# A two-layer encoder trunk in float32 on one NeuronCore: end keys first in the linear attention, opening weight sums begun at the fetch, the last input pair in two parts, and weight pairs in groups of three, four and four

## The chip, the core and the metric

The kernel runs on one core of a Trainium2 chip. TensorE (PE) multiplies, VectorE (DVE), ScalarE (ACT) and GpSimd (POOL) do the element-wise work, SyncE (SP) and POOL issue transfers. The metric is the device time of one execution in microseconds (us), all weights being read from HBM in that time.

## The reference

Two layers, each made of a feed-forward block, a mixer and a second feed-forward block, on 512 tokens plus 16 meta tokens (T = 528; the last feed-forward block has 512):

```python
for l in range(DEPTH):
    h = h + 0.5 * swiglu(rmsnorm(h, norm_gains[l, 0]), ffn_w_gate[l, 0], ffn_w_up[l, 0], ffn_w_down[l, 0])
    h = h + mixer(rmsnorm(h, norm_gains[l, 1]), w_in[l], ...)
    h = h + 0.5 * swiglu(rmsnorm(h, norm_gains[l, 2]), ffn_w_gate[l, 1], ffn_w_up[l, 1], ffn_w_down[l, 1])
return rmsnorm(h, final_norm)[:, N_META:]

def swiglu(x, w_gate, w_up, w_down):
    return (jax.nn.silu(x @ w_gate) * (x @ w_up)) @ w_down
```

The model width is 1024, the hidden width 2816. One half of the mixer is a gated linear attention (GLA) in two directions d, with 4 heads of 64 keys. It needs, for each direction, the running sum `bcum` of the log gates within a chunk, and from it three decayed copies of queries and keys:

```python
q_dec = qc * jnp.exp(bcum)
k_inv = kc * jnp.exp(-bcum)
k_end = kc * jnp.exp(btot - bcum)
kv_chunk = jnp.einsum('bhnjd,bhnjv->bhndv', k_end, vc)
```

`k_end` are the end keys of the title. The other half of the mixer is softmax attention, and both are merged by gates.

## The kernel before, in words

**Data.** `h` stays in SBUF, as 8 chunks of 128 features by 528 tokens. All weights are float32; each 128x1024 weight tile is split into a rounded part `whi` (ACT, L238) and a rest `wlo` (DVE, L239), and each product of a weight tile is three matmuls (hi by hi, hi by lo, lo by hi). A matmul of 264 tokens takes 0.122 us where PE doesn't wait.

**Feed-forward block.** The text calls the four blocks ffn(0,0), ffn(0,1), ffn(1,0), ffn(1,1) (layer, place in the layer); in names they read `_00_`, `_01_`, `_10_`, `_11_`. The 2816 hidden features are 11 "pairs" of 256. Gate and up projection of a pair are made by a Strassen-like scheme: the weights are cut in blocks 11, 12, 21, 22 and the inputs in two halves of the features and two of the tokens; seven products, named "1" to "7", of 24 matmuls each take the place of eight. Products 1, 2 and 4 use blocks 11, 12 and 22 as they are. The others use sums of blocks, made by transfers that add: s3 (for product 7) is the negative of block 11 (ACT, L189) plus block 21; s2 (product 6, the tile `w22`) is block 22 plus s3; s1 (product 5, the tile `w21`) is block 21 plus block 22; s4 (product 3) is the negative of block 12 plus s2. The adds are issued by POOL (L194), strictly one behind the other; an add that waits holds the queue behind it. Plain loads are issued by SP, in order as well. s1 and s2 have 2 buffers (`wsb`), s3 and s4 have 3 (`wsa`), raw weights 3, `whi` and `wlo` 4 each. Weights are split 4 tiles ahead of use (`make`) and loaded 6 ahead (`fetch`); the sums of a pair are ordered when its block 11 ("1") and 12 ("2") are split (`sums`, L196).

**Inputs of a block.** Each two chunks of the input form an input pair with 7 positions in `xc` (`Norm.pair`, L475), in the order of PLACE: products 1, 2, 5, 6, 7, 4, 3. Position 0 and 1 are plain halves, the others sums and differences made by DVE and split by ACT and DVE. The fourth pair (chunks 6, 7) is the last to come, since the previous phase makes the chunks of `h` in order (`add_to_h`, L529: two DVE operations, L527 and L536, or one, L532).

**Order of the products.** `ffn_steps` (L51) writes it by hand, by groups of pairs GROUPS. A block that isn't the first opens with products 1 and 2 of pair 0 together (step O, `two_products`, L566, with the last input pair left for the end), then products 1 and 2 of pair 1, then 6, 5, 7, 4, 3 of pair 0, and 6, 5 of pair 1 between. Behind each group come the down products of its hidden tiles (step D, L404), for 8 output chunks m; the last group's down products end the block, and after each the chunk m is added to `h` and handed to the next phase's norm. The row norm `rs` is got beside the opening and is needed first when hidden values are made. Which operation stands first on an engine is then decided by a scheduler that follows the program order and priorities.

**Linear attention.** `gla_pair` (L699) runs four times (2 layers, 2 pairs of heads), each for d = 0 and 1: a matmul z on PE (L721), Abs, Exp and Ln on ACT, the gate (DVE, L727), the running sum (DVE scan, L731), differences with the chunk's middle and end (L739 to L742), four exponentials on ACT, then three products on DVE and one on POOL: `qp` (L757), `kp` on POOL (L758), the end keys `ke` (L760), and the queries `qin` (L777). PE transposes `ke` (L764, L765); behind that DVE copies it (L767, L769). PE fills the time with the projections of the next tiles (L404), which stand between z and the transposes in its queue.

Of the kernel before, what the change touches and what calls it, by code (L numbers as in the profile page):

```python
# [17 lines left out]
P = 128  # L18
# [21 lines left out]
O_QB, O_KB, O_VB, O_GA, O_GB = 1568, 2080, 2208, 2336, 3360  # L40


GROUPS = (4, 4, 3)
HELD = 4
LATE = KC - 3
PLACE = {p: i for i, p in enumerate("1256743")}
# [112 lines left out]
class Weights:  # L159
# [32 lines left out]
    def add(self, t, src):  # L192

        self.nc.gpsimd.dma_start(t, src, accum_op=ALU.add)  # L194

    def sums(self, f, i, product, w):  # L196


        got = self.summed
        if product == "1":  # L200
            s3 = self.negative(f, i, "s3", w)
            self.add(s3, self.dram(f, i, "21"))
            s2 = self.block(f, i, "22", self.short, "wsb")
            self.add(s2, s3)
            got[f, i, "7"], got[f, i, "6"] = s3, s2
        else:
            s1 = self.block(f, i, "21", self.short, "wsb")
            self.add(s1, self.dram(f, i, "22"))
            s4 = self.negative(f, i, "s4", w)
            self.add(s4, got[f, i, "6"])  # L210
            got[f, i, "5"], got[f, i, "3"] = s1, s4
# [12 lines left out]

    def make(self, upto):
        nc = self.nc
        while self.made < min(upto, len(self.loads)):
            self.fetch(self.made + 1)
            s = self.made
            load = self.loads[s]  # L230
            w = self.raws.pop(s, None)
            if w is None:
                w = self.summed.pop(load)
            hi = self.hi_pool.tile([P, SLAB], F32R, tag="whi", name=f"whi{s}")
            lo = self.lo_pool.tile([P, SLAB], F32R, tag="wlo", name=f"wlo{s}")
            for a in np.split(np.arange(SLAB), 2 if s == 0 else 1):
                cs = slice(a[0], a[-1] + 1)
                nc.scalar.copy(hi[:, cs], w[:, cs])  # L238
                nc.vector.tensor_tensor(lo[:, cs], w[:, cs], hi[:, cs].bitcast(F32), ALU.subtract)  # L239
            self.got[s] = (hi, lo)  # L240
            self.got.pop(s - 12, None)
            self.made += 1
            if not isinstance(load, int) and load[2] in ("1", "2"):
                self.sums(*load, w)

    def use(self, j):
# [26 lines left out]
def build(tc, ctx, xt, wts, win, par, w2, const, umask, out):  # L273
# [7 lines left out]
        return ctx.enter_context(tc.tile_pool(name=name, bufs=bufs, space=space))  # L281

    one = pool("one", 1)
    slots = {n: pool("s_" + n, b) for n, b in dict(g=16, t=6, rs=2).items()}
# [68 lines left out]
    def v2(ap):  # L353
        return ap.rearrange("p (a b) -> p a b", a=2)
# [81 lines left out]
    class Norm:  # L436
# [38 lines left out]
        def pair(self, j):  # L475
# [15 lines left out]
            if not begun:  # L491
                parts(0, b11)
                parts(1, b21)
            S.activation(hi[:, 6], b22, AF.Copy, scale=-1.0)
            V.scalar_tensor_tensor(lo[:, 6], b22, -1.0, hi[:, 6].bitcast(F32), ALU.mult, ALU.subtract)
# [4 lines left out]
            V.tensor_tensor(t34[:, :w], b12, b22, ALU.subtract)  # L500
            V.tensor_tensor(t34[:, w:], b21, t12[:, w:], ALU.subtract)
            parts(slice(4, 6), v2(t34))

        def chunk(self, c):
# [12 lines left out]

# [22 lines left out]
    def ffn(l, f, norm, done, following):  # L540
# [25 lines left out]
        def two_products(p, names):  # L566
# [132 lines left out]
    def gla_pair(l, p, lr, w2t, sr, qa, ka, va, n_out):  # L699
# [17 lines left out]
        for d in range(2):  # L717
# [13 lines left out]
                V.tensor_tensor_scan(c[:, bs], ones.broadcast_to([P, n]), g[:, bs], 0.0, ALU.mult, ALU.add)  # L731
            mid = blk(c)[:, :, 63:64].broadcast_to([P, NB, P])
            tot = blk(c)[:, :, 127:128].broadcast_to([P, NB, P])
            mm_, mt_ = c[:, T - 1 : T].broadcast_to([P, META]), None
            src = c
            if d == 1:
                V.tensor_tensor(g, c, g, ALU.subtract)
                src = g
            V.tensor_tensor(blk(a), blk(src), mid, ALU.subtract)  # L739
            V.tensor_tensor(a[:, MB], src[:, MB], mm_, ALU.subtract)  # L740
            V.tensor_tensor(blk(ct_), blk(src), tot, ALU.subtract)
            V.tensor_copy(ct_[:, MB], a[:, MB])  # L742
            r16 = 1.0 / 16.0
            qp, kp = slot("p"), slot("p")
            if d == 0:
                S.activation(g, a, AF.Exp, scale=-r16)
                S.activation(a, a, AF.Exp, scale=r16)
                S.activation(c, c, AF.Exp, scale=r16)
                S.activation(ct_, ct_, AF.Exp, scale=-r16)
                ein, eq, ek, eend = c, a, g, ct_  # L750
            else:
                S.activation(c, a, AF.Exp, scale=-r16)
                S.activation(a, a, AF.Exp, scale=r16)
                S.activation(ct_, ct_, AF.Exp, scale=-r16)
                S.activation(g, g, AF.Exp, scale=r16)
                ein, eq, ek, eend = ct_, c, a, g
# [3 lines left out]
            V.tensor_tensor(ke, ka, eend, ALU.mult)  # L760

            tp = pair()
            for b, bs, _ in blocks:
                TE.transpose(tp[:, 0, bs], ke[:, bs], ident)  # L764
            TE.transpose(tp[:META, 1, :P], ke[:, MB], ident)  # L765
# [258 lines left out]
        norm.pools = open_pools("right", **{"x": dict(x=16), "xc": dict(xc=8)}[kind])  # L1024

    def block_pools():
        pools = open_pools("left", wsa=3, wsb=2)
        W.long, W.short = pools["wsa"], pools["wsb"]
        return pools

    def decay_weights(l):

        w, low = slot("t")[:, :512], slot("t")[:, :512]
        wt = one.tile([P, 512], F32R, tag="w2", name=nm("w2"))
        S.dma_start(w, w2[l])
        S.copy(wt, w)
        V.tensor_tensor(low, w, wt.bitcast(F32), ALU.subtract)
# [24 lines left out]
    def mixer(l, norm, done, following):  # L1062

        x, n_out = norm.x, T if l < DEPTH - 1 else SEQ
        pools = open_pools("left", e=8, i=5, p=7, q=6, k=5, lr=1)
# [210 lines left out]
```

## Time and profile before

| | us |
|---|---|
| median of three runs | 2263.21 |
| the three runs | 2260.45, 2263.21, 2268.38 |
| the profiled execution | 2263.49 |
| its span (first to last instruction) | 2261.6 |
| PE busy | 2204.5 (97%) |
| DVE busy | 1527.2 (68%) |
| ACT busy | 1218.3 (54%) |
| POOL busy | 164.7 (7%) |
| moved by transfers | 312.85 MB, 138 GB/s |

PE is busy nearly all the time, the other engines are not. The columns of the views are: start, duration, engine, line, operation, tiles; the bracket at the end of a row holds the idle time of that engine just before, and what ended it. The clock is shown as a share of full speed (1.00).

### The profile page before, as it was taken

The page shows a single profiled execution, that of the slowest core. Times are in us where ns is not written, and L with a number is a line of the kernel's source. Part 1 is how long each engine was busy: PE and PEld are TensorE (multiplying, and loading weights), DVE is VectorE, ACT ScalarE, POOL GpSimd, SP SyncE. Part 2 cuts the span into 40 slices and gives each one's busy share as a digit, 9 for nine tenths or more (in the row PEclk, how much of TensorE's full clock was granted, in tenths as well). Part 3 has the DMA queues.
Part 4 walks back from the last instruction along what each step waited for, and adds up shares of the span by engine and source line. Part 5 has one row for each costly group of instructions (what it writes and reads, how often), then busy time and mean ns, then how long its engine had stood idle before and what let it go on. Part 6 is the DMA issues. An engine that isn't in the chain of part 4 may idle for free. (4 is left out here: it accounts for less than half of the span.)

```text
span 2261.6 us, 39885 instructions
## 1 busy us (share of the span) xinstructions
PE 2204.5 (97%) x16538; PEld 2102.9 (93%) x16538; DVE 1527.2 (68%) x2397; ACT 1218.3 (54%) x1824; POOL 164.7 (7%) x184
## 2 busy tenths in 40 slices
PE   8999999999999999999979999999999999999998
PEld 8999999989999999999979999998888888989897
DVE  7657567577876666565676565575789767756565
ACT  8536355344784564453565363454557836636354
POOL 1011000000000010101011010100000000101010
PEclk9999999999999999999999999999999999999999
DMA  8778463211113485867658585732121135869661
GB/s 239 188 177 212 134 168 108 75 57 57 48 38 113 124 203 154 197 174 173 180 139 207 139 217 149 178 105 87 56 68 54 47 121 152 215 155 225 156 181 66
DMA packets 87542, 312.85 MB, mean 138 GB/s; under 512 B 9664, under 2 KB 11840, under 8 KB 87360
## 3 DMA queue, kind: packets, MB, share of 16 engines
q1 hardware_dynamic: 60816, 217.67, 28.6%
q0 software_dynamic: 24768, 90.19, 22.5%
q8 instruction: 130, 2.13, 0.4%
q10 hardware_dynamic: 1776, 2.43, 0.3%
q14 instruction: 52, 0.43, 0.1%
HBM read 263.07 MB, written 2.10 MB: 117 GB/s over the span
## 5 line engine op out<-in xcount | busy, mean ns | idle before, releaser
L597 PE MATMUL ss<-xc,whi 128*128 128x264 f32 (+1 forms) x4720 | 865.1, 285 | 16.9 <-ACT whi L238 9.5
L597 PEld LDWEIGHTS ss<-xc,whi 128*128 128x128 f32 x4720 | 734.7, 189 | 19.7 <-ACT whi L238 10.3
L597 PE MATMUL ss<-xc,wlo 128*128 128x264 f32 (+1 forms) x2360 | 671.4, 285 | 5.1 <-DVE wlo L239 5.1
L404 PE MATMUL ss<-g,whi 128*128 128x264 f32 (+1 forms) x2620 | 482.8, 300 | 0.0
L597 PEld LDWEIGHTS ss<-xc,wlo 128*128 128x128 f32 x2360 | 446.8, 189 | 6.4 <-DVE wlo L239 6.3
L404 PEld LDWEIGHTS ss<-g,whi 128*128 128x128 f32 x2620 | 380.6, 188 | 15.7
L404 PE MATMUL mm<-x,whi 128*128 128x264 f32 (+1 forms) x1712 | 385.8, 315 | 0.0
L238 ACT CAST whi<-w 128x1024 fp32r<-128x1024 f32 (+1 forms) x220 | 230.0, 1046 | 266.2 <-PE ss L404 116.1
L239 DVE TENSOR_TENSOR wlo<-w,whi 128x1024 fp32r<-128x1024 f32 (+1 forms) x220 | 266.6, 1218 | 116.1 <-ACT whi L238 114.8
L238 ACT CAST whi<-raw 128x1024 fp32r<-128x1024 f32 x190 | 199.2, 1048 | 260.2 <-PE ss L597 89.8
L239 DVE TENSOR_TENSOR wlo<-raw,whi 128x1024 fp32r<-128x1024 f32 x190 | 232.1, 1222 | 105.8 <-ACT whi L238 104.8
L404 PE MATMUL ss<-g,wlo 128*128 128x264 f32 (+1 forms) x1310 | 302.2, 300 | 0.0
L404 PEld LDWEIGHTS mm<-x,whi 128*128 128x128 f32 x1712 | 281.2, 190 | 15.3 <-DVE x L393 0.2
L404 PE MATMUL mm<-x,wlo 128*128 128x264 f32 (+1 forms) x856 | 265.2, 314 | 0.0
L404 PEld LDWEIGHTS ss<-g,wlo 128*128 128x128 f32 x1310 | 209.2, 188 | 8.3
L239 DVE TENSOR_TENSOR wlo<-s,whi 128x1024 fp32r<-128x1024 f32 x86 | 105.1, 1222 | 95.7 <-ACT whi L238 95.6
L238 ACT CAST whi<-s 128x1024 fp32r<-128x1024 f32 x86 | 90.3, 1050 | 146.9 <-PE ss L597 128.3
L404 PEld LDWEIGHTS mm<-x,wlo 128*128 128x128 f32 x856 | 161.2, 190 | 7.6
L527 DVE SCALAR_TENSOR_TENSOR t<-ss,rs 128x528 f32<-128x528 f32 (+1 forms) x93 | 64.6, 700 | 126.4 <-PE ss L404 126.3
L189 ACT ACTIVATE s<-w 128x1024 f32<-128x1024 f32 x86 | 91.2, 1060 | 81.7 <-DMA w<-win 46.5
L194 POOL DMA_DIRECT2D w<-win x43 | 37.8, 880 | 599.3 <-DVE wlo L239 222.3
L393 DVE TENSOR_TENSOR g<-c,g 128x528 fp32r<-128x528 f32 (+1 forms) x88 | 61.5, 699 | 22.6 <-ACT g L392 22.6
(280 smaller groups left out, 2829.6 us busy)
## 6 DMA issues: line engine op xcount, KB each, us to landing
w<-win SPq DMA_DIRECT2D x218, 512.0 KB, 4.7
raw<-wts SPq DMA_DIRECT2D x190, 512.0 KB, 3.3
w<-win POOLq DMA_DIRECT2D x43, 512.0 KB, 6.8
s<-win POOLq DMA_DIRECT2D x43, 512.0 KB, 6.7
w<-s POOLq DMA_DIRECT2D x43, 512.0 KB, 5.9
s<-w POOLq DMA_DIRECT2D x43, 512.0 KB, 7.0
h<-xt SPq DMA_DIRECT2D x3, 528.0 KB, 7.6
out<-h SPq DMA_DIRECT2D x2, 512.0 KB, 2.9
```

The costliest lines, as they stand in the source:

```text
L189: self.nc.scalar.activation(t, w, AF.Copy, scale=-1.0)
L194: self.nc.gpsimd.dma_start(t, src, accum_op=ALU.add)
L238: nc.scalar.copy(hi[:, cs], w[:, cs])
L239: nc.vector.tensor_tensor(lo[:, cs], w[:, cs], hi[:, cs].bitcast(F32), ALU.subtract)
L393: V.tensor_tensor(lo, src, hi.bitcast(F32), ALU.subtract)
L404: TE.matmul(acc.half[i][:width], lhs, rhs[:, acc.spans[i]], start=first, stop=last)
L527: V.scalar_tensor_tensor(cut(dst[rows]), pv[rows], -0.5 * f, cut(rs[rows]), ALU.mult, ALU.mult)
L597: TE.matmul(acc[:, j], a[:, j, k], b[:, at], start=bool(begin and k == 0 and i == 0), stop=k == len(x) - 1 and i == 2, skip_group_check=no ...
```

## The change

Four parts, with some buffers moved. The line numbers of the changed kernel are higher by 25 to 60 than those of before.

1. GROUPS becomes (3, 4, 4): the last group of each block has four pairs, so each of its down chunks has 48 matmuls instead of 36.
2. In `gla_pair` the end keys' own difference, exponential and product come first and with priority, and PE's transposes of them stand behind them in the program; the other differences follow. For d = 1 the end keys need no difference with the chunk's end. `kp` goes from POOL to DVE. The tile of the gates' weights goes to a pool of its own.
3. Weight sums, in the three blocks that open with step O: those of pair 0 are ordered when its blocks 11 and 12 are fetched, not when they are split. Of pair 1, s3 is begun when block 11 is split, the negative of block 12 when block 12 is; s2 and the add to s4 are ordered when pair 0's product 6 is split, s1 when pair 0's product 5 is. `wsa` has 4 buffers instead of 3.
4. The last input pair: at chunk 7 only positions 0 and 1 are made, from `h` directly (`early`); the rest and the squares of chunks 6 and 7 follow behind the opening's step O in the program (`late`). In `pair`, position 6 is made last. `rs` has one buffer instead of 2.

```diff
-GROUPS = (4, 4, 3)
+GROUPS = (3, 4, 4)
...
+    def fourth(self, f, i, w=None):
+        if w is not None:
+            self.summed[f, i, "3"] = self.negative(f, i, "s4", w)
+        if (f, i, "6") in self.summed:
+            self.add(self.summed[f, i, "3"], self.summed[f, i, "6"])
...
     def sums(self, f, i, product, w):
...
+        opening = f != (0, 0)
+        if product == "1" and not (opening and i == 0):
+            self.third(f, i, w)
+            if not (opening and i == 1):
+                self.second(f, i)
+        elif product == "2" and not (opening and i == 0):
+            if not (opening and i == 1):
+                self.first(f, i)
+            self.fourth(f, i, w)
+        elif product == "6" and opening and i == 0:
+            self.second(f, 1)
+            self.fourth(f, 1)
+        elif product == "5" and opening and i == 0:
+            self.first(f, 1)
...
-                self.raws[self.fetched] = self.block(*load[:2], DIRECT[load[2]])
+                w = self.raws[self.fetched] = self.block(*load[:2], DIRECT[load[2]])
+                if load[0] != (0, 0) and load[1:] == (0, "1"):
+                    self.third(*load[:2], w)
+                    self.second(*load[:2])
+                    self.first(*load[:2])
+                elif load[0] != (0, 0) and load[1:] == (0, "2"):
+                    self.fourth(*load[:2], w)
...
+        def early(self, j):
+
+            hs = slice(0, live[0] // 2)
+            hi, lo = self.seven()
+            self.x.append((hi, lo))
+            for r in range(2):
+                S.activation(hi[:, r], h(2 * j + r, hs), AF.Identity, scale=col(self.gc + 2 * j + r))
+                V.scalar_tensor_tensor(lo[:, r], h(2 * j + r, hs), col(self.gc + 2 * j + r), hi[:, r].bitcast(F32),
+                                       ALU.mult, ALU.subtract)
+
+        def late(self):
+            self.pair(KC // 2 - 1)
+            for c in (KC - 2, KC - 1):
+                self.square(c)
...
         def chunk_of_pair(self, c):
-            if c % 2 and c < KC - 1:
+            if c < KC - 2:
                 self.square(c)
-            if c % 2:
+            if c == KC - 1:
+                self.early(c // 2)
+            elif c % 2:
                 self.pair(c // 2)
-            if c == KC - 1 or c % 2 == 0:
-                self.square(c)
...
+            norm.late()
             for name in names:
                 finished(p, name)
...
+            ke = slot("p")
             src = c
-            if d == 1:
-                V.tensor_tensor(g, c, g, ALU.subtract)
-                src = g
+            with tc.high_priority():
+                if d == 0:
+                    V.tensor_tensor(blk(ct_), blk(c), tot, ALU.subtract)
+                    V.tensor_tensor(ct_[:, MB], c[:, MB], last, ALU.subtract)
+                    S.activation(ke, ct_, AF.Exp, scale=-r16)
+                else:
+                    V.tensor_tensor(g, c, g, ALU.subtract)
+                    S.activation(ke, g, AF.Exp, scale=r16)
+                    src = g
+                V.tensor_tensor(ke, ka, ke, ALU.mult)
+            tp = pair()
+            for b, bs, _ in blocks:
+                TE.transpose(tp[:, 0, bs], ke[:, bs], ident)
...
-            G.tensor_tensor(kp, ka, ek, ALU.mult)
-            ke = slot("p")
-            V.tensor_tensor(ke, ka, eend, ALU.mult)
...
+            V.tensor_tensor(kp, ka, ek, ALU.mult)
...
-        pools = open_pools("left", wsa=3, wsb=2)
+        pools = open_pools("left", wsa=4, wsb=2)
```

**Where instructions move.** POOL's adds in the opening of ffn(0,1), before; `s3_01_1` is s3 of pair 1, `w22_01_1` its s2, `w21_01_1` its s1, `s4_01_1` its s4, and `win` the weights in HBM:

```order
L194 DMA s3_01_1_9249<-win 128x1024
L194 DMA w22_01_1_9252<-s3_01_1_9249 128x1024
L194 DMA w21_01_1_9346<-win 128x1024
L194 DMA s4_01_1_9349<-w22_01_1_9252 128x1024
L194 DMA s3_01_2_9623<-win 128x1024
```

The same place in the changed kernel:

```order
L194 DMA s3_01_1_9250<-win 128x1024
L194 DMA w22_01_1_9332<-s3_01_1_9250 128x1024
L194 DMA s3_01_2_9627<-win 128x1024
L194 DMA s4_01_1_9325<-w22_01_1_9332 128x1024
L194 DMA w21_01_1_9415<-win 128x1024
```

s1's add now stands behind s4's, which reads the s2 that the add ahead of it still has to land; it stood ahead of it. ffn(1,1) has the same order. In ffn(1,0) the changed order is s3, s2, s3 of pair 2, s1, s4: there s1 stays ahead of s4.

DVE in the linear attention, layer 0, first pair of heads, d = 1, before: from the end of the running sum (L731) to the end keys' product (L760; `i264` are the keys, `t294` the sum without its own gate, L737, `ss` and `mm` are PSUM):

```order
L731 SCALAR_TENSOR_TENSOR t295_4962<-const_84,t294_4961 128x16
L239 TENSOR_TENSOR wlo109_5210<-raw35_4838,whi109_5209 128x1024
L737 TENSOR_TENSOR t294_4961<-t295_4962,t294_4961 128x528
L527 SCALAR_TENSOR_TENSOR i342_5265<-mm343_5266,rs245_4513 128x264
L739 TENSOR_TENSOR t293_4960<-t294_4961,t295_4962 128x512
L740 TENSOR_TENSOR t293_4960<-t294_4961,t295_4962 128x16
L741 TENSOR_TENSOR t296_4963<-t294_4961,t295_4962 128x512
L742 COPY t296_4963<-t293_4960 128x16
L757 TENSOR_TENSOR p297_4978<-i261_4654,t295_4962 128x528
L527 SCALAR_TENSOR_TENSOR i342_5265<-mm344_5267,rs245_4513 128x264
L777 TENSOR_TENSOR p290_4951<-i261_4654,t296_4963 64x528
L760 TENSOR_TENSOR p299_4986<-i264_4713,t294_4961 128x528
```

The same place in the changed kernel, to the end keys' product (now L788):

```order
L772 SCALAR_TENSOR_TENSOR t295_4965<-const_84,t294_4964 128x16
L264 TENSOR_TENSOR wlo109_5213<-raw35_4841,whi109_5212 128x1024
L785 TENSOR_TENSOR t294_4964<-t295_4965,t294_4964 128x528
L567 SCALAR_TENSOR_TENSOR i342_5268<-mm343_5269,rs245_4516 128x264
L793 TENSOR_TENSOR t293_4963<-t294_4964,t295_4965 128x512
L788 TENSOR_TENSOR p297_4976<-i264_4716,p297_4976 128x528
```

Six operations between scan and product are gone from there (they follow later). On PE the transposes move up as well: between z's matmuls and the transposes stood 74, 88, 81, 92 matmuls in the four GLA steps of layer 0 and 51, 98, 41, 63 in layer 1; in the changed kernel it is 67, 70, 67, 82 and 36, 80, 41, 39.

DVE in the opening of ffn(1,0), before, from the last chunk's addition to `h` on (L527 scales the down product, L536 adds it; L489, L495 and L497 to L501 make the last input pair `xc1060`):

```order
L527 SCALAR_TENSOR_TENSOR t1056_13402<-ss1055_13365,rs867_9503 128x528
L454 TENSOR_TENSOR t1021_13080<-t1021_13080,t1054_13362 128x528
L536 TENSOR_TENSOR h_82<-h_82,t1056_13402 128x528
L489 TENSOR_TENSOR xc1060_13410<-t1057_13405,xc1059_13409 128x264
L497 TENSOR_TENSOR t1061_13417<-t1057_13405 128x264
L498 TENSOR_TENSOR t1061_13417<-t1058_13406,t1061_13417 128x264
L500 TENSOR_TENSOR t1062_13418<-t1057_13405,t1058_13406 128x264
L489 TENSOR_TENSOR xc1060_13410<-t1058_13406,xc1059_13409 128x264
```

The same place in the changed kernel (L567 and L576 are the scaling and the addition, L540 makes positions 0 and 1 from `h`):

```order
L567 SCALAR_TENSOR_TENSOR t1055_13400<-ss1054_13344,rs867_9507 128x528
L540 SCALAR_TENSOR_TENSOR xc1057_13404<-h_82,par_83,xc1056_13403 128x264
L576 TENSOR_TENSOR h_82<-h_82,t1055_13400 128x528
L264 TENSOR_TENSOR wlo249_13423<-w12_10_1_13291,whi249_13422 128x1024
L540 SCALAR_TENSOR_TENSOR xc1057_13404<-h_82,par_83,xc1056_13403 128x264
L520 TENSOR_TENSOR t1062_13489<-t1060_13485 128x264
L523 TENSOR_TENSOR t1063_13490<-t1060_13485,t1061_13486 128x264
```

The two plain positions now come right behind the additions, and the sums and squares behind them.

More of the change, by code (lines that the diff above doesn't have):

```diff
@@ L194, in add, with third, second, first @@
         self.nc.gpsimd.dma_start(t, src, accum_op=ALU.add)
-    def sums(self, f, i, product, w):
[L199 to L211, printed above, removed]
+    def third(self, f, i, w):
+        s3 = self.summed[f, i, "7"] = self.negative(f, i, "s3", w)
+        self.add(s3, self.dram(f, i, "21"))
+    def second(self, f, i):
+        s2 = self.summed[f, i, "6"] = self.block(f, i, "22", self.short, "wsb")
+        self.add(s2, self.summed[f, i, "7"])
+    def first(self, f, i):
+        s1 = self.summed[f, i, "5"] = self.block(f, i, "21", self.short, "wsb")
+        self.add(s1, self.dram(f, i, "22"))
+    def fourth(self, f, i, w=None):
[3 more added lines that the diff above has]
+            self.add(self.summed[f, i, "3"], self.summed[f, i, "6"])
+    def sums(self, f, i, product, w):
+        opening = f != (0, 0)
[12 more added lines that the diff above has]
+            self.first(f, 1)
     def fetch(self, upto):
@@ L242, in make @@
             self.made += 1
-            if not isinstance(load, int) and load[2] in ("1", "2"):
+            if not isinstance(load, int):
                 self.sums(*load, w)
@@ L283, in build @@
     one = pool("one", 1)
-    slots = {n: pool("s_" + n, b) for n, b in dict(g=16, t=6, rs=2).items()}
+    slots = {n: pool("s_" + n, b) for n, b in dict(g=16, t=6, rs=1).items()}
     small = pool("small", 4)
@@ L502, in pair @@
             parts(slice(4, 6), v2(t34))
+            S.activation(hi[:, 6], b22, AF.Copy, scale=-1.0)
+            V.scalar_tensor_tensor(lo[:, 6], b22, -1.0, hi[:, 6].bitcast(F32), ALU.mult, ALU.subtract)
         def chunk(self, c):
@@ L754, in gla_pair @@
                 S.activation(ct_, ct_, AF.Exp, scale=-r16)
-                S.activation(g, g, AF.Exp, scale=r16)
-                ein, eq, ek, eend = ct_, c, a, g
+                ein, eq, ek = ct_, c, a
             V.tensor_tensor(qp[:, :n_out], qa, eq[:, :n_out], ALU.mult)
-            G.tensor_tensor(kp, ka, ek, ALU.mult)
-            ke = slot("p")
[L760 to L765, printed above, removed]
+            V.tensor_tensor(kp, ka, ek, ALU.mult)
             for hh in range(2):
@@ L1033, in decay_weights @@
         w, low = slot("t")[:, :512], slot("t")[:, :512]
-        wt = one.tile([P, 512], F32R, tag="w2", name=nm("w2"))
+        wt = slots["w2"].tile([P, 512], F32R, tag="w2", name=nm("w2"))
         S.dma_start(w, w2[l])
@@ L1064, in mixer @@
         x, n_out = norm.x, T if l < DEPTH - 1 else SEQ
-        pools = open_pools("left", e=8, i=5, p=7, q=6, k=5, lr=1)
+        pools = open_pools("left", e=8, i=5, p=7, q=6, k=5, lr=1, w2=1)
         banks = open_pools("left", psum=("mm", "sm"), mm=2, sm=2)
```

16 lines of the change are left out of this document (7 added, 9 removed).

## The prediction

> **What bounds the kernel now.** I read the page first, then the windows of the places that the change touches, then what PE waited for, then the timelines there.
>
> ```profile
> span 2261.6 us, 39885 instructions
> PE 2204.5 (97%) x16538; PEld 2102.9 (93%) x16538; DVE 1527.2 (68%) x2397; ACT 1218.3 (54%) x1824; POOL 164.7 (7%) x184
> ```
>
> PE is idle for at most 57 us of the span; only there, and where its clock is low, can time be gained. The windows (PE, weight loads, DVE, ACT, POOL busy; granted clock; transfers' share; GB/s) are the linear attention of layer 0, the openings of ffn(0,1), ffn(1,0), ffn(1,1), and a stretch inside ffn(1,0):
>
> ```profile
> 428.00:512.00 84.00, 76.85 (x590) 72.08 (x589) 63.76 (x132) 39.57 (x81) 8.02 (x4) 0.96 0.18 57
> 786.00:826.00 40.00, 37.77 (x290) 36.72 (x289) 25.94 (x38) 27.15 (x36) 5.23 (x6) 0.96 0.74 190
> 1147.00:1195.00 48.00, 36.24 (x262) 34.79 (x261) 33.31 (x53) 28.22 (x42) 5.26 (x6) 0.89 0.55 134
> 1895.00:1940.00 45.00, 40.51 (x310) 38.44 (x309) 30.95 (x44) 29.99 (x41) 5.21 (x6) 1.00 0.76 185
> 1195.00:1500.00 305.00, 305.00 (x2505) 305.00 (x2504) 188.80 (x235) 147.16 (x177) 28.76 (x33) 1.00 0.67 172
> ```
>
> Inside a block PE never waits: 305.00 of 305 us. Regrouping and moved sums are worth nothing there, as long as the sums stay on time. What is left are the openings and the attention; PE's waits say the same:
>
> ```profile
> PE ss L764 <- DVE p L760: 12.5, 8, 2.1
> PE ss L597 <- ACT whi L238: 9.5, 4, 4.7
> PE ss L597 <- ACT snap L608: 7.4, 4, 3.8
> ```
>
> The first row is the end keys; the others are weights or PSUM tiles that come late in openings.
>
> **End keys first (part 2).** The worst of the eight waits, with what DVE did ahead of it:
>
> ```profile
> 453.47 0.63 PE L764 MATMUL ss<-const,p 128*128 128x128 f32 x4 [2.13 <-DVE p L760]
> ```
>
> ```profile
> 444.19 1.44 DVE L731 TENSOR_TENSOR_SCAN t<-const,t 128x128 f32<-128x128 f32 x5
> 445.55 1.20 DVE L239 TENSOR_TENSOR wlo<-raw,whi 128x1024 fp32r<-128x1024 f32 x1
> 446.67 0.70 DVE L737 TENSOR_TENSOR t<-t,t 128x528 f32<-128x528 f32 x1
> 450.42 0.42 DVE L527 SCALAR_TENSOR_TENSOR i<-mm,rs 128x264 f32<-128x264 f32 x1
> 451.61 1.72 DVE L760 TENSOR_TENSOR p<-i,t 128x528 f32<-128x528 f32 x1
> ```
>
> From the sum's end (445.6) to the product's end (453.3) it takes 7.7 us. In the new order there remain wlo 1.20, L737 0.70, one L527 0.42, one difference (as L737, 0.70) and the product, at the eight's median:
>
> ```profile
> L760 DVE TENSOR_TENSOR p<-i,t x8: 696/706/1715, 438.9 to 1641.1; 128x528 f32<-128x528 f32 x8
> ```
>
> That is 3.7 us: the product ends 4.0 us earlier (ACT's exponential lies beside the two rows in between). But PE's cover shrinks too: 88 matmuls become 70, and one takes 73.11/600 = 0.122 us:
>
> ```profile
> 1294.14 73.11 PE ss L597 x600
> ```
>
> so PE arrives 2.2 us earlier. For d = 1 I add 0.9 us: the step before now has kp on DVE (0.71) behind the transposes, ahead of this step's gate. 2.13 - 4.0 + 2.2 + 0.9 leaves 1.2. The other seven, worked the same way from their rows of the order, leave 0.4, 0.4 and 0.7 in layer 0 and 1.0, 0, 0 and about 3.2 in layer 1 (there the cover falls from 63 to 39): 6.9 of 12.5 us, a gain of 5.6. Then the clock:
>
> ```profile
> 455.25:458.66 3.41, 3.41 (x17) 3.17 (x16) 2.36 (x7) 0.00 (x0) 0.00 (x0) 0.50 0.49 154
> ```
>
> After that gap of 2.13 us the clock was 0.50 for 3.41 us, which costs 1.7 us; the first window's mean clock of 0.96 leaves room for two (2 x 1.7 = 3.4 of 84 us). With gaps of 1.2 us I expect them mostly gone, one perhaps coming back in layer 1: 2.4 us. Part 2 gains 8.0; its bounds are 2 (transposes move up as far as the product does, and only the slow product's 1.0 and some clock is won) and 15.9 (all 12.5 and both dips).
>
> A rule speaks against the clock term. The Trainium skill, "TensorE: Matmul & The Clock Gate", Part 1 ("What's actually happening"), has the clock halved only after an idle window of about 3.4 us; by it gaps near 2 us cost no clock, part 2 would gain 5.6, and the clock in my term for ffn(1,1) below would go too. The trace disagrees: its dip stands behind 2.13 us.
>
> **Weight sums (part 3): ffn(0,1).** POOL and ACT in its opening:
>
> ```profile
> 802.47 0.88 POOL L194 DMA_DIRECT2D w<-s  x1 [19.51 <-DMA w<-win]
> 804.81 0.87 POOL L194 DMA_DIRECT2D w<-win  x1 [1.47 <-DVE wlo L239]
> 811.50 0.86 POOL L194 DMA_DIRECT2D s<-w  x1 [5.82 <-DMA w<-s]
> ```
>
> ```profile
> 814.26 1.04 ACT L238 CAST whi<-w 128x1024 fp32r<-128x1024 f32 x1 [2.27 <-DMA w<-win]
> 815.21 0.59 ACT L608 COPY snap<-ss 128x528 f32<-128x528 f32 x1
> ```
>
> s2 of pair 1 is added at 802.47, s1 at 804.81, s4 at 811.50, waiting 5.82 us for s2 to land. ACT waits for s1 too, 2.27 us, and behind that cast stands the snap on which PE's next product of pair 0 waits. In the new order s1 is behind s4, so it waits for s2's landing. s2 lands alone now. The page's medians of such adds:
>
> ```profile
> w<-win POOLq DMA_DIRECT2D x43, 512.0 KB, 6.8
> w<-s POOLq DMA_DIRECT2D x43, 512.0 KB, 5.9
> ```
>
> and the add to s3 of pair 2, issued beside s4's here, took longer:
>
> ```profile
> s<-win POOLq DMA_DIRECT2D x1, 512.0 KB, 8.1
> ```
>
> s2 lands between 802.47 + 5.9 = 808.4 and, as now, just before 811.50; s1 issues some 1.1 us later (two POOL issues), 809.5 to 812.1, and lands 6.8 to 8.1 us on, 816.3 to 820.2, against 814.2. The cast, the snap and PE's product come 2 to 6 us later: 4.0, and 0.5 for a longer dip (one stands here already, window clock 0.96). Cost 4.5, from 2 to 7.7 with a further dip.
>
> **ffn(1,1).** The same order, with PE's own wait:
>
> ```profile
> 1913.55 0.85 POOL L194 DMA_DIRECT2D w<-s  x1 [19.68 <-DVE c L615]
> 1916.21 0.86 POOL L194 DMA_DIRECT2D w<-win  x1 [1.81 <-DVE wlo L239]
> 1922.97 0.88 POOL L194 DMA_DIRECT2D s<-w  x1 [5.90 <-DMA w<-s]
> ```
>
> ```profile
> 1926.29 1.04 ACT L238 CAST whi<-w 128x1024 fp32r<-128x1024 f32 x1 [2.84 <-DMA w<-win]
> ```
>
> ```profile
> 1927.88 0.50 PE L597 MATMUL ss<-xc,whi 128*128 128x256 f32 x2 [1.56 <-ACT snap L608]
> ```
>
> s1 issues at 1920.5 to 1923.5 and lands 6.8 to 8.1 later, 1927.3 to 1931.6 against 1926.2: 1 to 5 us, 3.3 taken. No dip now (clock 1.00); PE's waits grow to some 5 us, above those with a dip: 1.7. Cost 5.0, from 1 to 7.9 (5 and 2.9 of clock, what the dip in ffn(1,0) costs, below).
>
> **Groups, two-part input: ffn(1,0).** Its PE waits:
>
> ```profile
> 1148.44 0.41 PE L597 MATMUL ss<-xc,whi 128*128 128x264 f32 x2
> ...
> 1152.55 0.39 PE L597 MATMUL ss<-xc,wlo 128*128 128x264 f32 x1 [2.24 <-DVE wlo L239]
> 1165.87 0.51 PE L597 MATMUL ss<-xc,whi 128*128 128x264 f32 x2 [1.70 <-ACT snap L608]
> 1178.14 0.51 PE L597 MATMUL ss<-xc,whi 128*128 128x264 f32 x2 [2.23 <-ACT whi L238]
> 1183.35 0.81 PE L597 MATMUL ss<-xc,whi 128*128 128x264 f32 x2 [4.70 <-ACT whi L238]
> ```
>
> ```profile
> 1184.00:1189.00 5.00, 5.00 (x24) 5.00 (x24) 1.60 (x3) 0.00 (x0) 0.00 (x0) 0.50 0.99 290
> ```
>
> ```profile
> 1157.92 0.70 DVE L527 SCALAR_TENSOR_TENSOR t<-ss,rs 128x528 f32<-128x528 f32 x1
> ```
>
> PE begins the block at 1148.4, DVE scales the last chunk only at 1157.92: it is 9.5 us behind. The last four down chunks have 36 matmuls each; with 48 they take 12/36 more, and
>
> ```profile
> 1238.56 4.40 PE ss L404 x36
> ```
>
> gives 4 x 1.47 = 5.9 us in which DVE catches up (no cost: the total of down products is the same, an earlier group has fewer). The first two waits, 3.9 us together, are DVE's lag; I take 2.4 of them off, since the opening now also needs the early positions of chunks 6 and 7. The last two, 6.9, hang on s1, whose load waits for a buffer that DVE's wlo frees; DVE is up to 5.9 earlier there, PE 2.4: I take 3.0 off. The dip behind (1183.35 to 1189 at 0.50, 2.9 us lost) stays. Gain 5.4, from 9 down to a loss of 1, since s1 has s3 of pair 2 ahead of it now.
>
> The rest I cost at nothing: pair 0's sums, and the sums inside blocks, are covered by the 305 us without a gap; kp on DVE is 8 x 0.71 us on an engine that PE waits for only at the places counted, and the slow product of 1.72 beside POOL's kp counts once, in the case above. The single rs buffer is free when its last reader, DVE at 1157.92, is done, before the squares are, from which the next rs is made; and rs itself is read only at the hidden values, two products behind. Were that cover gone, the hidden values of pair 0 would be late, which shows at pair 0's PSUM tiles.
>
> **Sum.** 2263.5 (profiled execution, 0.3 above the median) - 8.0 - 5.4 + 4.5 + 5.0 = 2259.6. A measurement here tells 0.3%, 6.8 us, from no change: faster is below 2256.4, slower above 2270.0.
>
> **Rivals.**
> - *The turned adds hardly bind.* For it: without s1 beside it, s2 may land in less than its 5.9, and pair 2's load stands earlier on SP. Against: at both places s1 was already late by 2.27 and 2.84. Then they cost 1.0 each: 2263.5 - 8.0 - 5.4 + 2.0 = 2252.1. 30%.
> - *The transposes' wait moves along.* The scheduler put them earlier by 7 to 24 matmuls at seven of eight places. Part 2 gains 2: 2265.6. It speaks against it that the chain is shortened by more than the cover in the case worked above. 20%.
> - *Slower: POOL's queue holds everything behind s2.* Both turned places at their upper ends, 7.7 and 7.9, and in ffn(1,0) s1 is held by s3 of pair 2, whose negative ACT makes late, so the gain of 5.4 is lost: 2263.5 - 8.0 + 15.6 = 2271.1. For it: transfers are busy 0.74 and 0.76 of the time there. It decides once s2's add takes over 8 us alone. 17%.
> - The forecast: 33%. That the change doesn't do what it says is excluded for the orders quoted.
>
> **How the numbers follow.** Faster: most of the first rival and the lower end of the forecast, 0.35. Slower: most of the last, and the upper ends, 0.19. Same: 0.46. Both signs stay open, but the forecast alone would span 2253 to 2268 (part 2's, ffn(1,0)'s and the adds' bounds, not all at once). The range takes in the first rival with more of part 2's 15.9, to 2248, and the slower one with the loss of 1, to 2273.
>
> **What would show it.** Right: the end keys' wait near 7 us over eight with clock 1.00 in layer 0's attention; in both turned openings s1's add behind s4's, and the cast of it 2 to 6 us later against pair 0's products; ffn(1,0) with some 6 us of waits where it had 11.8. Wrong: s1 landing before ACT asks for it; waits of the end keys at 12 us again; a new PE gap inside a block, above all at the second pair of a group; or a longer tail after the last down product.

## The result, and the profile after

The changed kernel takes 2315.74 us (median of five runs, 2311.17 to 2316.11), against 2261.89 (median of five, 2260.45 to 2268.38): a ratio of 1.0224, interval 1.0206 to 1.0243. It is some 54 us slower, where 2259.6 was forecast.

The page of the changed kernel, span and engines:

```profile
span 2312.0 us, 39845 instructions
PE 2220.9 (96%) x16556; PEld 2118.4 (92%) x16556; DVE 1518.3 (66%) x2405; ACT 1214.2 (53%) x1824; POOL 150.7 (7%) x176
```

The span grew by 50.4 us. PE is idle for 91.1 us of it where it was 57.1, 34.0 more, and busy for 16.4 more with the same products, so its clock was lower for longer (its mean is 0.982 where it was 0.992). The windows, the attention of layer 0 first, then a stretch inside ffn(1,0):

```profile
428.00:512.00 84.00, 81.97 (x660) 77.54 (x658) 61.00 (x134) 42.66 (x83) 0.00 (x0) 1.00 0.20 64
...
1215.00:1500.00 285.00, 275.71 (x2220) 274.86 (x2219) 170.48 (x212) 130.78 (x158) 28.81 (x33) 0.98 0.67 171
```

The attention is what the change meant it to be: PE busy 81.97 of 84 us where it was 76.85, clock 1.00. The block's inside, without a gap before, now loses 9.3 us in 285. What PE waited for:

```profile
PE ss L638 <- ACT snap L649: 60.3, 18, 7.4
...
PE ss L791 <- DVE t L794: 2.0, 4, 0.6
...
PE ss L791 <- DVE p L788: 1.3, 4, 0.6
```

The transposes of the end keys (L791) wait 3.3 us over eight times where it was 12.5. What grew is one row, the snap of ACT (the copy that takes a product out of PSUM): 60.3 us in 18 waits, 7.4 in 4 before. Five of the 18:

```profile
60.99 0.51 PE L638 MATMUL ss<-xc,whi 128*128 128x264 f32 x2 [1.18 <-ACT snap L649]
...
822.16 0.81 PE L638 MATMUL ss<-xc,whi 128*128 128x264 f32 x2 [7.39 <-ACT snap L649]
...
944.67 0.81 PE L638 MATMUL ss<-xc,whi 128*128 128x264 f32 x2 [4.29 <-ACT snap L649]
...
1202.85 0.81 PE L638 MATMUL ss<-xc,whi 128*128 128x264 f32 x2 [5.29 <-ACT snap L649]
...
1958.99 0.80 PE L638 MATMUL ss<-xc,whi 128*128 128x256 f32 x2 [7.14 <-ACT snap L649]
```

The waits at 61, 822, 1203 and 1959 are in the four openings, 21.0 us together; the other 39.3 us, in 14 waits, lie inside the blocks, such as the one at 944.67 in ffn(0,1). There, ACT's rows:

```profile
932.48 2.00 ACT L263 CAST whi<-w 128x1024 fp32r<-128x1024 f32 x2
934.42 1.06 ACT L263 CAST whi<-s 128x1024 fp32r<-128x1024 f32 x1
935.38 0.59 ACT L649 COPY snap<-ss 128x528 f32<-128x528 f32 x1
943.07 1.06 ACT L189 ACTIVATE s<-w 128x1024 f32<-128x1024 f32 x1 [7.10 <-DMA w<-win]
944.03 0.58 ACT L649 COPY snap<-ss 128x528 f32<-128x528 f32 x1
```

and SP's load for which the negative (L189) waits, and its time to landing:

```profile
934.81 0.33 SPq L184 DMA_DIRECT2D w<-win  x1
```

```profile
w<-win SPq DMA_DIRECT2D x1, 512.0 KB, 8.2
```

ACT stands 7.10 us in front of the negative of block 12 of pair 6. Its tile is loaded only from 934.81 on, when one of the three raw buffers is free, and lands 8.2 us later. The snap that PE waits for stands behind it. It is so at all 14 places: ACT's row ahead of the snap is each time the negative of a block 12 (of pair 5, 6, 9 or 10), after 3.31 to 7.19 us of waiting for its load, and never the cast of a sum. The order of ACT's queue shows that this place is new. Before:

```
L238 CAST whi191_10954<-s4_01_4_10674 128x1024
L608 COPY snap930_10952<-ss929_10923 128x528
L189 ACTIVATE s3_01_6_11059<-w11_01_6_10990 128x1024
L608 COPY snap931_10982<-ss923_10786 128x528
...
L238 CAST whi195_11099<-s3_01_5_10822 128x1024
L392 CAST g934_11051<-c926_10854 128x528
L387 ACTIVATE c926_10854<-c926_10854 128x528
L189 ACTIVATE s4_01_6_11139<-w12_01_6_11065 128x1024
```

and in the changed kernel:

```
L263 CAST whi189_10850<-s4_01_4_10549 128x1024
L649 COPY snap930_10848<-ss929_10819 128x528
L189 ACTIVATE s4_01_6_11035<-w12_01_6_10961 128x1024
L649 COPY snap931_10878<-ss918_10576 128x528
```

With three buffers the negative s4 of pair 6 takes the buffer of s3 of pair 5, which is free once that is split (`whi195`, then its `wlo`), and stands behind that. With four it takes the buffer of s4 of pair 4, free after `whi189`, and stands right there, some ten rows earlier and ahead of snap931. The waits of all 86 negatives say it from the other side; before:

```profile
  DMA w<-win: 46.5, 19
  DVE wlo L239: 35.2, 43
```

after:

```profile
  DMA w<-win: 164.9, 56
  DVE wlo L264: 0.7, 1
```

The wait for a buffer (43 times) is gone; the wait for the load has taken its place.

### The profile page after: what moved, and what is told of

It is laid out like the page before. It is cut to its first block, busy times and chain, and to the rows that moved or that the text cites. A ratio compares the mean times of both kernels' runs of the same rounds, so it can differ in the third digit from the quotient of the medians.

```text
span 2312.0 us, 39845 instructions
## 1 busy us (share of the span) xinstructions
PE 2220.9 (96%) x16556; PEld 2118.4 (92%) x16556; DVE 1518.3 (66%) x2405; ACT 1214.2 (53%) x1824; POOL 150.7 (7%) x176
## 4 chain that ended last, share of the span: by engine, by line
PE 72%; DMA 10%; DVE 8%; ACT 6%; issue 3%; POOL 0%; SPq 0%; DVEq 0%; ACTq 0%; POOLq 0%
PE ss L429 25%; PE ss L638 24%; PE mm L429 13%; DMA w<-win 9%; DVE wlo L264 3%; PE sm L429 2%; ACT whi L263 2%; PE sm L1020 1%; ACT snap L649 1%; PE ss L995 1%; PE ss L1204 1%; PE ss L620 1%; ACT t L412 1%; PE sm L1036 1%; PE ss L996 1%
## 5 line engine op out<-in xcount | busy, mean ns | idle before, releaser
L638 PE MATMUL ss<-xc,whi 128*128 128x264 f32 (+1 forms) x4720 | 885.6, 289 | 62.5 <-ACT snap L649 60.3
L638 PEld LDWEIGHTS ss<-xc,whi 128*128 128x128 f32 x4720 | 751.1, 193 | 67.9 <-ACT snap L649 64.8
L638 PE MATMUL ss<-xc,wlo 128*128 128x264 f32 (+1 forms) x2360 | 680.3, 288 | 1.7 <-DVE wlo L264 1.7
L638 PEld LDWEIGHTS ss<-xc,wlo 128*128 128x128 f32 x2360 | 456.2, 193 | 2.4 <-DVE wlo L264 2.4
L189 ACT ACTIVATE s<-w 128x1024 f32<-128x1024 f32 x86 | 91.0, 1058 | 165.5 <-DMA w<-win 164.9
L567 DVE SCALAR_TENSOR_TENSOR t<-ss,rs 128x528 f32<-128x528 f32 (+1 forms) x93 | 64.9, 700 | 82.2 <-PE ss L429 82.0
L661 DVE TENSOR_TENSOR c<-snap,ss 128x528 f32<-128x528 f32 (+1 forms) x43 | 29.9, 696 | 92.5 <-ACT snap L649 92.5
```

Of the source, the lines that this page charges most:

```text
L189: self.nc.scalar.activation(t, w, AF.Copy, scale=-1.0)
L567: V.scalar_tensor_tensor(cut(dst[rows]), pv[rows], -0.5 * f, cut(rs[rows]), ALU.mult, ALU.mult)
L638: TE.matmul(acc[:, j], a[:, j, k], b[:, at], start=bool(begin and k == 0 and i == 0), stop=k == len(x) - 1 and i == 2, skip_group_check=no ...
L661: V.tensor_tensor(st["c"][:, :, 3], st["r"], st["Z"][:, :, :w], ALU.add)
```

## The experiments

Theory A: the fourth buffer of `wsa` lets the negatives of block 12 move ahead on ACT, where they wait for loads in front of the snaps. Rivals: B, the new groups make the waits (loads and sums meet at other pairs); C, the sums begun early fill the queues; and, for the waits inside blocks, POOL's order in place of ACT's. Ratios are to the kernel before, run beside each; its medians there were 2265.93, 2264.78 and 2266.39 us.

**b_wsa4**, the fourth buffer alone (the other three edits only make room for it):

```diff
-    slots = {n: pool("s_" + n, b) for n, b in dict(g=16, t=6, rs=2).items()}
+    slots = {n: pool("s_" + n, b) for n, b in dict(g=16, t=6, rs=1).items()}
...
-        pools = open_pools("left", wsa=3, wsb=2)
+        pools = open_pools("left", wsa=4, wsb=2)
...
-        wt = one.tile([P, 512], F32R, tag="w2", name=nm("w2"))
+        wt = slots["w2"].tile([P, 512], F32R, tag="w2", name=nm("w2"))
...
-        pools = open_pools("left", e=8, i=5, p=7, q=6, k=5, lr=1)
+        pools = open_pools("left", e=8, i=5, p=7, q=6, k=5, lr=1, w2=1)
```

> The kernel before, with four buffers for s3 and s4 instead of three and nothing else of the change but the room for it (one rs buffer, the gates' weights in a pool of the mixer). Theory A (the fourth buffer lets the negative of block 12 move ahead on ACT, in front of the snap that frees PE's PSUM tile, and it waits there for a load): PE waits for snap L608 at the second and later pairs of the groups, 30 us or more in total where it was 7.4, the clock dips behind the longer waits, and the time is 30 to 55 us above 2262. Theory B (the new groups make the stall, since loads and sums meet at other pairs) and theory C (sums begun early in the openings fill the queues): within 5 us of 2262.

Measured: 2318.35 us, ratio 1.0236 (1.0206 to 1.0267). Its waits:

```profile
PE ss L597 <- ACT snap L608: 45.8, 19, 6.0
PE ss L764 <- DVE p L760: 13.4, 8, 2.3
```

The fourth buffer alone makes the loss, with the old groups, sums and attention. B and C fall.

**b_groups**, GROUPS alone:

```diff
-GROUPS = (4, 4, 3)
+GROUPS = (3, 4, 4)
```

> The kernel before with GROUPS (3, 4, 4) and nothing else. Theory A: no new wait inside a block; the last down chunks of a block are longer, so the opening of ffn(1,0) waits up to 5 us less: 2257 to 2263. Theory B (the groups make the stall): PE waits for snap L608 for 30 us or more, time 2295 to 2315. Theory C: as A.

Measured: 2259.19 us, ratio 0.9969 (0.9955 to 0.9984), about 7 us faster.

```profile
PE ss L597 <- ACT snap L608: 5.7, 4, 2.9
PE ss L597 <- ACT whi L238: 4.9, 3, 3.6
PE ss L597 <- DVE wlo L239: 3.7, 6, 0.8
```

No new wait inside blocks; the late weights cost 4.9 and 3.7 us where it was 9.5 and 5.1.

**a_wsa3**, the changed kernel with three buffers:

```diff
-        pools = open_pools("left", wsa=4, wsb=2)
+        pools = open_pools("left", wsa=3, wsb=2)
```

> The changed kernel with three buffers for s3 and s4. The negatives of block 12 then stand on ACT where they stood before, and in the openings s1's add stands ahead of s4's again. Theory A: the waits inside blocks vanish (from some 39 us of gaps and 25 of clock), the two openings lose their waits of 7 us, and what is left is the gain of the attention and of ffn(1,0): 2240 to 2252. Theory B or C: the waits inside blocks stay, and the time stays above 2290.

Measured: 2245.09 us, ratio 0.9918 (0.9890 to 0.9946).

```profile
PE ss L638 <- ACT snap L649: 8.9, 4, 2.8
```

One number, 4 to 3, turns 54 us lost into some 19 gained. The single `rs` buffer and the moved tile of the gates' weights are still in this kernel, so they don't make the loss. But the number turns two queues: in the openings s1's add (the first row) stands ahead of s4's (the second) again, as before the change.

```profile
791.29 0.88 POOL L194 DMA_DIRECT2D w<-win  x1 [1.43 <-DMA w<-win]
794.95 0.86 POOL L194 DMA_DIRECT2D s<-w  x1 [2.78 <-DMA w<-s]
```

So in the changed kernel the turned adds, too, come with the fourth buffer. The next run parts ACT's queue from POOL's.

**a_pin**, four buffers, the negative queued behind the cast of its own tile (`issue_after` orders the queue, without a wait):

```diff
-            self.summed[f, i, "3"] = self.negative(f, i, "s4", w)
+            with self.tc.issue_after(self.cast) if self.pinned else nullcontext():
+                self.summed[f, i, "3"] = self.negative(f, i, "s4", w)
...
+            self.pinned = True
             self.fourth(f, i, w)
+            self.pinned = False
...
-                nc.scalar.copy(hi[:, cs], w[:, cs])
+                self.cast = nc.scalar.copy(hi[:, cs], w[:, cs]).ins
```

> The changed kernel, four buffers, where the negative of block 12 is queued on ACT behind the cast of the same tile; POOL's order is as in the changed kernel, in the two openings and at the second pairs of the groups. Theory A: the waits inside blocks vanish, the waits of 7 us in the openings of ffn(0,1) and ffn(1,1) stay, with their dips: 2255 to 2270. If POOL's order (s4 ahead of s1 at the second pairs of a group) makes the waits inside blocks and not ACT's: they stay, above 2290.

Measured: 2250.38 us, ratio 0.9936 (0.9913 to 0.9960), below the expected 2255.

```profile
PE ss L642 <- ACT snap L653: 16.1, 3, 7.6
```

The negatives wait for loads less (164.9 us in the changed kernel):

```profile
  DMA w<-win: 18.6, 10
```

The waits inside blocks are gone with POOL's order unchanged, so it was ACT's queue. 16.1 us are left; all but 1.3 are the openings of ffn(0,1) and ffn(1,1):

```profile
807.87 0.81 PE L642 MATMUL ss<-xc,whi 128*128 128x264 f32 x2 [7.58 <-ACT snap L653]
```

```profile
1909.95 0.80 PE L642 MATMUL ss<-xc,whi 128*128 128x256 f32 x2 [7.18 <-ACT snap L653]
```

**a_pool**, the changed kernel with s4's add behind s1's in the openings:

```diff
             self.second(f, 1)
-            self.fourth(f, 1)
         elif product == "5" and opening and i == 0:
             self.first(f, 1)
+            with self.tc.issue_after(self.last):
+                self.fourth(f, 1)
```

> The changed kernel with one turn undone: in the openings s4's add of pair 1 is queued on POOL behind s1's. The negatives stay ahead on ACT. If the two causes are separate and add up: the waits of 7.4 and 7.1 us in the openings of ffn(0,1) and ffn(1,1) fall to 2 to 3 each, with less of the dips behind, 10 to 16 us off 2316; the waits inside blocks stay at some 39 us: 2300 to 2306. Rival: the opening's wait comes from the negatives on ACT as well, then it stays at 7 us and the time within 4 us of 2316.

Measured: 2310.18 us, ratio 1.0200 (1.0177 to 1.0223). Less than expected: the median lies 5.6 us below the changed kernel's, and the two ratios' intervals overlap. PE's waits for the snap are 57.2 us, those of the two openings 5.42 and 4.84. The add behind which s1 waited was not all.

**a_pin_pool**, both edits, four buffers.

> The changed kernel with both turns undone: four buffers, the negative of block 12 queued on ACT behind the cast of its tile, and in the openings s4's add of pair 1 behind s1's. If the two causes are all of the loss: the waits of 7.6 and 7.2 us left in the run with the negative put back fall to 2 to 3, with the dips of 3.4 us each: 2250 less 12 to 17, 2233 to 2240, below the run with three buffers (2245). Rival: s4, added later, is then late for product 3, and a wait appears there: 2243 to 2250.

Measured: 2245.39 us, ratio 0.9913 (0.9900 to 0.9926): not the 2233 to 2240. It lies in the range of the rival, but no wait for s4 appears in the two openings; PE still waits 5.31 and 5.08 us for the snap in the two openings. In the opening of ffn(0,1), POOL's rows, then the landings of the last two:

```profile
796.58 0.88 POOL L194 DMA_DIRECT2D w<-s  x1 [20.55 <-DVE wlo L268]
798.24 0.88 POOL L194 DMA_DIRECT2D s<-win  x1 [0.78 <-ACT s L189]
798.88 1.13 POOL L194 DMA_DIRECT2D w<-win  x1
```

```profile
s<-win POOLq DMA_DIRECT2D x1, 512.0 KB, 8.6
w<-win POOLq DMA_DIRECT2D x1, 512.0 KB, 11.6
```

s1's add (the last) is early now, but that to s3 of pair 2 goes just ahead of it, and s1 lands only after 11.6 us. The next run turns these two.

**a_pin_pool_s3**, the same, with the add to s3 of pair 2 queued behind s1's:

```diff
-            self.third(f, i, w)
+            if opening and i == 2:
+                s3 = self.summed[f, i, "7"] = self.negative(f, i, "s3", w)
+                with self.tc.issue_after(self.last):
+                    self.add(s3, self.dram(f, i, "21"))
+            else:
+                self.third(f, i, w)
```

> The changed kernel with four buffers, both turns undone, and in the openings the add to s3 of pair 2 queued on POOL behind s1's of pair 1. In the run before it that add ran beside s1's, whose landing took 11.7 us where it took 9.1 with three buffers. If the two adds hinder each other: s1 lands in some 9 us, the waits of 5.3 and 5.1 us in the two openings fall to 2.5 to 3, and the ratio to 0.988 to 0.990. Rival: s1's landing is as slow alone, and the waits stay at 5 us: 0.991 to 0.993.

Measured: 2241.3 us, ratio 0.9897 (0.9880 to 0.9913), the lowest ratio of all; its interval overlaps those of the kernels with three buffers. In the openings POOL's adds stand as they did before the change. s1 lands in less, and the first opening's wait falls to 2.26:

```profile
w<-win POOLq DMA_DIRECT2D x1, 512.0 KB, 8.6
```

```profile
802.99 0.51 PE L648 MATMUL ss<-xc,whi 128*128 128x264 f32 x2 [2.26 <-ACT snap L659]
```

**b_gla**, the changed `gla_pair` put into the kernel before, nothing else:

> The kernel before with the changed linear attention alone (end keys first, kp on DVE). The prediction's term: 8.0 us gained, end keys' waits 6.9 us left of 12.5. Rival, by what the other runs show (under 4 us of waits left, no dip in the attention): 11 to 14 us gained, 2248 to 2251. Rival, the wait moves along: 2 us gained.

Measured: 2253.14 us, ratio 0.9945 (0.9929 to 0.9960): 12.5 us gained, interval 9 to 16.

```profile
PE ss L750 <- DVE t L753: 1.9, 4, 0.6
PE ss L750 <- DVE p L747: 1.4, 4, 0.5
```

The waits fall to 3.3 us, and the clock in the attention's window is 1.00. The end keys' product takes 709 ns at most where it took 1715 once; that one, from 451.61 to 453.33, ran while POOL's kp did (450.91 to 452.76):

```profile
L747 DVE TENSOR_TENSOR p<-i,p x8: 699/702/709, 443.2 to 1629.8; 128x528 f32<-128x528 f32 x8
```

**b_early**, the two-part input pair alone (`early`, `late`, `pair` and `chunk_of_pair` as changed):

> The kernel before with the last input pair in two parts alone. The prediction gave the two parts no gain of their own (the 5.4 us in ffn(1,0) came from the longer down chunks): within 3 us of before. Rival: the early positions let PE begin the opening sooner, and the first waits of ffn(1,0) (2.24 and 1.70) go: 3 to 5 us gained.

Measured: 2273.14 us, ratio 1.0041 (1.0022 to 1.0061), outside both expectations. In ffn(1,0) two new waits for the inputs, 1.43 and 2.91 us, stand where before PE waited 2.24 us for `wlo` and 1.70 for the snap; the later ones for the weights stay (1.61 and 5.54 where it was 2.23 and 4.70):

```profile
PE ss L613 <- ACT xc L514: 2.9, 1, 2.9
```

**b_sums**, the new `sums` and `fetch` alone, three buffers:

> The kernel before with the sums begun at the fetch and in the new order, three buffers, nothing else. The prediction costed pair 0's sums at nothing and pair 1's order at a loss; with three buffers s1's add stands ahead of s4's: within 0.3% of before. Rival: the sums of pair 1, ordered later, land later at the openings: 2 to 8 us slower.

Measured: 2263.72 us, ratio 0.9996 (0.9982 to 1.0010). Nothing.

**b_groups_gla**, groups and attention together, neither sums nor two-part pair:

> The kernel before with the new groups and the changed linear attention, without the sums and without the two-part input pair. The two alone gave ratios of 0.9969 and 0.9945. If they add up: 0.9914, as low as the changed kernel with three buffers (0.9918), and the sums and the two-part pair are worth nothing together. Rival: the gains overlap or the sums carry part of the gain: 0.994 to 0.997.

Measured: 2245.43 us, ratio 0.9917 (0.9902 to 0.9932), close to the product of the two alone, 0.9914.

**a_wsa3_noearly**, the changed kernel with three buffers, the two-part pair undone:

> The changed kernel with three buffers and without the two-part input pair, that is groups, linear attention and sums. If the two-part pair costs here what it costs alone (ratio 1.0041): 0.986 to 0.990, the fastest. Rival: it pays where the down chunks are longer and the sums early: 0.992 to 0.996.

Measured: 2244.17 us, ratio 0.9913 (0.9898 to 0.9928). Between the two expectations: no faster than with the two-part pair (0.9918), which so costs nothing here, and pays nothing.

## Why the prediction was wrong, point by point

**Sums inside blocks and the fourth buffer, costed at nothing: the step that failed.** The prediction argued that PE never waits inside a block, and that the moved sums are worth nothing there "as long as the sums stay on time". They did stay on time: none of the 14 waits inside blocks stands behind the cast of a sum. But the fourth buffer, which the change lists, has no term in the prediction and isn't named there. A buffer more changes the place of an instruction on another engine: the wait for a buffer had kept the negative of block 12 behind the snaps. The order of ACT's queue in the changed kernel already shows it; the orders quoted ahead of the prediction are those of POOL, PE and DVE at the places of the change, not ACT's inside the blocks. Shown by b_wsa4 (1.0236 for the buffer alone), a_wsa3 (0.9918 without it) and a_pin (0.9936 with it, the negative put back). The sign named as a refutation, a new PE gap inside a block, is what came, though not at the second pair of a group: the negatives are those of the third and fourth.

**End keys first: right, undersized.** 8.0 us forecast, 12.5 measured (9 to 16); 6.9 us of waits expected to stay, 3.3 did, and the clock came back. The longest single wait is 0.6 where 1.2 and 3.2 were forecast, so the allowances, the 0.9 us for kp and the shorter cover, were too big together; which of them wasn't tried. The rival "the transposes' wait moves along" fell. The low clock behind gaps near 2 us went with the gaps (the window's clock from 0.96 to 1.00). The waits give 9.2 us of the 12.5, and two dips of 1.7, for which the window's mean clock leaves room, give the rest, so the trace's account stands and that of the Trainium skill, "TensorE: Matmul & The Clock Gate", Part 1 ("What's actually happening"), without clock, falls short; the interval alone wouldn't exclude it.

**Longer down chunks, ffn(1,0): right for the chunks alone.** 5.4 forecast; b_groups gained 7 (3.6 to 10.2) with nothing else changed. Its waits in ffn(1,0) are 5.6 us where 11.8 stood and some 6 were forecast; the longest:

```profile
1177.23 0.51 PE L597 MATMUL ss<-xc,whi 128*128 128x264 f32 x2 [3.65 <-ACT whi L238]
```

In the changed kernel they are 8.0, of which 5.29 is the wait at 1202.85; ACT's cast ahead of that snap waited 5.67 us for its weights. In a_pin this wait is gone.

**The turned adds: right in kind; the size stays open.** POOL's rows of the changed kernel in ffn(0,1):

```profile
804.52 0.88 POOL L194 DMA_DIRECT2D w<-s  x1 [20.25 <-DVE wlo L264]
806.13 0.88 POOL L194 DMA_DIRECT2D s<-win  x1 [0.74 <-ACT s L189]
810.01 0.86 POOL L194 DMA_DIRECT2D s<-w  x1 [3.00 <-DMA w<-s]
810.63 1.14 POOL L194 DMA_DIRECT2D w<-win  x1
```

and ACT's cast of s1, with the snap behind it:

```profile
820.56 1.04 ACT L263 CAST whi<-w 128x1024 fp32r<-128x1024 f32 x1 [8.40 <-DMA w<-win]
821.51 0.59 ACT L649 COPY snap<-ss 128x528 f32<-128x528 f32 x1
```

s1 issued at 810.63 (809.5 to 812.1 forecast), and landed just before 820.56, 9.9 us on where 6.8 to 8.1 was taken. PE waited 7.39 us where 0.90 and 0.75 stood, and in ffn(1,1) 7.14 where 1.63, 0.76 and 1.56 stood: 8.9 us more, against 4.0 and 3.3 of waits in the forecast, 9.5 with the clock. In time it is less sure. From a_pin to a_pin_pool_s3, which has the order of before, the two places' waits fall from 7.58 and 7.18 to 2.26 and 2.52, and the ratio by 0.0039, some 9 us; the two intervals just touch. From a_pin to a_wsa3, which has s1 ahead of s4 too, the ratio falls by 0.0018 only, some 4 us, and the intervals overlap. Of the 0.0039 the turned pair has 0.0023 and the add to s3 of pair 2, which stands ahead as well and which the forecast had only for ffn(1,0), 0.0016; the intervals overlap. The rival that they hardly bind fell, and the slower rival had the right queue but not the size: POOL's order doesn't reach the 54 us.

**The sum of what was priced.** a_pin holds all of it, the turned adds too: 0.9936, or 14.5 us gained, where the net of the terms was 3.9. So they were pessimistic by some 11 us: 4.5 of it in the end keys, 1.6 in ffn(1,0). If the parts add up, as groups and attention do, the rest is the turned adds, at some 5 us in place of 9.5; that isn't shown. What was missed is the step from 0.9936 to 1.0224, some 65 us: 39.3 us of waits inside the blocks, the one of 5.29 in the opening of ffn(1,0), and the clock behind them (mean 0.982 where a_pin has 0.994).

**Open.** Why the two-part pair alone costs 0.4%: its profiled execution (2266.49 us) was the quickest of six, so its trace doesn't hold the typical loss, and with longer down chunks it costs nothing. It wasn't tried whether a fourth raw buffer, which would let the load land ahead of the negative, also cures the waits.

## What to carry to other kernels

A buffer added to a pool isn't free where queues run in order: the wait for a buffer may be what holds an instruction behind a more urgent one, and once it is gone the instruction moves ahead and waits there, for something slower. Ahead of such a change, compare the order on every engine that writes or reads that pool, in the middle of the longest loop too, and ask of each instruction that moved up what it waits for and who is queued behind it. Where more buffers are wanted, pin the order; here four buffers with the order pinned were no faster than three, clear of noise.

## What the runs showed of the hardware

The clock of PE doesn't follow from the length of a gap alone. In a_wsa3 PE waited 2.85 us in the opening of ffn(0,1) and 2.29, with a wait of 0.30 just ahead, in that of ffn(1,0):

```profile
802.11 0.51 PE L638 MATMUL ss<-xc,whi 128*128 128x264 f32 x2 [2.85 <-ACT snap L649]
```

```profile
1139.70 0.59 PE L638 MATMUL ss<-xc,whi 128*128 128x264 f32 x1 [2.29 <-ACT xc L539]
```

```profile
799.00:820.00 21.00, 18.15 (x149) 17.94 (x148) 13.08 (x17) 13.67 (x17) 2.59 (x3) 1.00 0.98 239
1138.74:1145.56 6.82, 5.86 (x26) 5.87 (x27) 6.82 (x14) 4.94 (x9) 0.00 (x0) 0.50 0.00 0
```

The longer one left the clock at 1.00; the shorter one lies at the start of 6.82 us at 0.50. The Trainium skill, "TensorE: Matmul & The Clock Gate", Part 1 ("What's actually happening"), says that the window over which activity is judged is free-running, about 3.4 us long; the stretches here are one or two of it (3.41 and 6.82 us), which agrees, while gaps shorter than one window sufficed, which its rule of one idle window doesn't give.

The add to s1 took 11.6 us in ffn(0,1) and 10.8 in ffn(1,1) just behind that to s3 of pair 2 (a_pin_pool), and 8.6 in both when only that order was turned (a_pin_pool_s3). In a_wsa3, where neither s3's nor s4's add stands just ahead either, it took 9.1 and 10.0. So adds that run side by side seem to hinder each other, but it isn't the only thing that sets the time; what else does is open.
